# A two-layer decoder trunk on one core: its setup written in another order

## The chip, the core and the metric

The kernel runs on one core of a Trainium2 chip, as one program without collectives. Its time is device microseconds (us) of one execution. TensorE multiplies matrices; VectorE (DVE in the profile), ScalarE (ACT) and GpSimd (POOL) do the elementwise work; SyncE (SP) and ScalarE issue the DMAs. Every engine works off its own instructions in the order in which they stand, and waits at an instruction until what it depends on is done. PEld are TensorE's weight loads, which run beside its matmuls.

## What is computed

The input is 512 tokens of width 1024, in float32. The reference normalises them and runs two layers on them:

```python
h = layer_norm(x, ln_in_g, ln_in_b)
for l in range(DEPTH):                       # 2
    mix = token_mix(h, positions, ...)       # pooling, convolution and sparse attention, gated and merged
    h = layer_norm(DEEPNORM_ALPHA * h + mix, ln1_g[l], ln1_b[l])
    ffn = conv_ffn(h, ...)
    h = layer_norm(DEEPNORM_ALPHA * h + ffn, ln2_g[l], ln2_b[l])
```

`token_mix` begins with one projection of h, whose columns are the inputs of all three branches. Among them are the key of a sparse-attention indexer and its eight query heads. Keys and queries are rotated by angles that come from `positions` (`rope`); the indexer scores every visible key for every query, and the 128 best are kept.

## The kernel before

A float32 product is done in three passes over a high and a low part: a value is copied to a rounded `hi` (ScalarE), the rest `lo = value - hi` is a subtraction, and hi·hi, lo·hi and hi·lo are added in PSUM (`proj`, lines L289, L290, L291). Weights come in 246 chunks of 128x1024 through `Weights`: a DMA into one of two `w_raw` buffers (L70), the copy `w_hi` on ACT (L74), the subtraction `w_lo` (L78) on DVE, or as two halves on POOL for chunks named in `W.side`. There are four hi/lo pairs. So chunk i+2 can be loaded once chunk i is split, and chunk i+4 can be split once TensorE is done with chunk i.

Tokens are four blocks of 128. `setup` does, block by block: statistics of x (`stats`), mean and variance, the power -0.5 on POOL (L177), the normalisation in two halves of 512 (L197), four transposes per half (L200), scale and shift into a tile `gbt` of the four-buffer pool `gb` (three of four on ACT, L208, the last on DVE, L205), then `hT_hi` on ACT (L212) and `hT_lo` on DVE (L112). After block 1 and after block 3 `mix_head.block` multiplies the last two blocks by the first three weight chunks: chunk 0 (indexer key, bank v), chunk 1 (attention key) and chunk 2 (pooling), banks s. 24 products of 256 columns per chunk and pair of blocks make 144. Last stand the rotation angles: positions, a chain of eleven small DVE operations, a sine on ACT, eight products that spread it over partitions, and the tables `sinT` (ACT) and `cosT` (DVE).

Layer 0 starts with `rotate` of the indexer key (`ki`), the attention key (`k`) and the four query tiles (`qi0` to `qi3`, chunks 3 to 6): ACT reads the product into `t` (L424, L425, L440, L455), issues four DMAs that swap halves (L405), POOL multiplies by `sinT` (L409), DVE by `cosT` (L408), and DVE adds (L410). Indexer scores follow (`mask`, L475, L477), then the top-128 search on DVE. Later each gate chunk frees its PSUM bank through DVE (L728).

The order on each engine is set by a list scheduler of the tile framework, which also adds the waits. `add_manual_dep(..., ISSUE_ORDER)` fixes the order of two instructions without a wait of its own. The scheduler reuses eight DMA completion counters (lanes, `DMAHW0` to `DMAHW7`): a DMA that takes a lane waits until the DMA that had it last has landed.

Of the kernel before, what the change touches and what calls it, by code (L numbers as in the profile page):

```python
# [15 lines left out]
P = 128  # L16
D = 1024
L = 512
NB = 4
# [35 lines left out]
class Weights:  # L55
    def __init__(self, tc, w, raw_pool, split_pool, look, nchunk):
        self.tc, self.nc, self.w = tc, tc.nc, w
        self.raw_pool, self.split_pool = raw_pool, split_pool
        self.look = look
        self.n = nchunk  # L60
        self.emitted = 0
        self.used = 0
        self.ready = []
        self.side = set()

    def emit(self, upto):
        nc = self.nc
        while self.emitted < min(upto, self.n):
# [21 lines left out]
def trunk_kernel(ctx, tc, x, positions, w, poolw, params, lnv, cons, out):  # L90
# [20 lines left out]
    def split_lo(lo, src, hi, eng=None):  # L111
        (eng or V).tensor_tensor(out=lo, in0=src, in1=hi.bitcast(F32), op=ALU.subtract)  # L112

# [1 line left out]
    h = const.tile([P, NB, D], F32, name="h")  # L115
    xv = x[0].rearrange("(b p) d -> p b d", p=P)
    par = const.tile([P, DEPTH, NPAR], F32, name="par")
    nc.scalar.dma_start(out=par[:, 0, PO_LN:NPAR], in_=params[:, 0, PO_LN:NPAR])
# [7 lines left out]
    cst = const.tile([P, 37], F32, name="cst")  # L126
    nc.scalar.dma_start(out=cst, in_=cons)
# [31 lines left out]
    class Norm:  # L159
        def __init__(self, i, last=False):  # L160
# [3 lines left out]
            self.tr = [None] * NB  # L164

# [5 lines left out]
        def apply(self, b):  # L171
# [5 lines left out]
            G.tensor_tensor(out=rs, in0=ve, in1=mhalf, op=ALU.pow)  # L177
# [17 lines left out]
            for half in range(2):  # L195
# [3 lines left out]
                for k in range(4):  # L199
                    self.tr[b] = T.transpose(pt[:, k * P:(k + 1) * P], hb[:, k * P:(k + 1) * P], ident)  # L200
                y = g_slot().rearrange("p (k t) -> p k t", k=4)
# [11 lines left out]
                split_lo(lo, y, hi, G if half in LN_POOL else V)  # L213
# [9 lines left out]
    class Head:  # L223
# [3 lines left out]

        def block(self, b):
            if self.wts is None:
                n = len(self.c0s)  # L230
                self.wts = [W.take(look=n - 1 - i) for i in range(n)]
                self.os = [bank(t) for t, _ in zip(("v", "s", "s"), self.c0s)]
            if b % 2 == 1:
                for o, wt, c0 in zip(self.os, self.wts, self.c0s):
                    in_part(o, wt, c0, max(c0, (b - 1) * P), (b + 1) * P)

    def setup():
        norm = Norm(0)
        for b in range(NB):
            for c in range(2):  # L240
                norm.stats(b, c)
            norm.apply(b)
            mix_head.block(b)
        V.tensor_scalar(half_par[:, :, 0:41], par[:, :, PO_B:PO_B + 41], 0.5, None, op0=ALU.mult)
        V.tensor_scalar(half_par[:, :, 41:45], par[:, :, PO_CG:PO_CG + 4], 0.5, None, op0=ALU.mult)
        with tc.tile_pool(name="rt", bufs=1) as rt:
            sel = rt.tile([P, NB, NB, 32], F32R, name="sel")
            G.tensor_copy(sel, ident.rearrange("p (b f) -> p b f", b=NB).unsqueeze(2).to_broadcast([P, NB, NB, 32]))
            pi = rt.tile([P, P], I32, name="pi")
            for b in range(NB):  # L250
                nc.sync.dma_start(out=pi[32 * b:32 * b + 32, :],
                                    in_=positions[:, b * P:(b + 1) * P].to_broadcast([32, P]))
            both = rt.tile([P, 2, P], F32, name="both")
            ang, cang = both[:, 0, :], both[:, 1, :]
            V.tensor_scalar(ang, pi, cst[:, 0:1], None, op0=ALU.mult)
            n = rt.tile([P, P], F32, name="n")
            magic = 12582912.0
            V.tensor_scalar(n, ang, 1.0 / (2 * PI), magic, op0=ALU.mult, op1=ALU.add)
            V.tensor_scalar(n, n, magic, None, op0=ALU.subtract)
            for c in (6.28125, 0.00193023681640625, 5.066394805908203e-06,  # L260
                      2 * PI - 6.28125 - 0.00193023681640625 - 5.066394805908203e-06):
                V.scalar_tensor_tensor(out=ang, in0=n, scalar=-c, in1=ang, op0=ALU.mult, op1=ALU.add)
            V.tensor_scalar(ang, ang, 3.1415925, -3.1415925, op0=ALU.min, op1=ALU.max)
            V.scalar_tensor_tensor(out=cang, in0=ang, scalar=-1.0, in1=ang, op0=ALU.mult, op1=ALU.min)
            V.tensor_scalar(cang, cang, PI / 2, None, op0=ALU.add)
            A.activation(both, both, AF.Sin)
            b_hi = rt.tile([P, 2, P], F32R, name="b_hi")
            b_lo = rt.tile([P, 2, P], F32R, name="b_lo")
            A.activation(b_hi, both, AF.Copy)
            split_lo(b_lo, both, b_hi)  # L270
            for half in range(2):
                o = bank("p").rearrange("p (b v t) -> p b v t", b=2, v=2)
                for b in range(2):
                    w = sel[:, 2 * half + b].rearrange("p r f -> p (r f)")
                    T.matmul(o[:, b], w, b_hi, start=True, stop=False)
                    T.matmul(o[:, b], w, b_lo, start=False, stop=True)
# [3 lines left out]
        return norm  # L280

    def proj(o, wt, col, xs, kts):
# [3 lines left out]
        for i, (wc, xc) in enumerate(kts):  # L286
# [4 lines left out]
            T.matmul(o, wl, xh(xc), start=False, stop=(i == n - 1))  # L291

    def in_part(o, wt, c0, a, b):
        proj(o[:, a - c0:b - c0], wt, 0,
             (lambda k: hT_hi[:, k, a:b], lambda k: hT_lo[:, k, a:b]),
# [620 lines left out]
```

## Time and profile before

| | us |
|---|---|
| median of 3 runs (1559.52 to 1560.57) | 1559.91 |
| profiled execution, first to last instruction | 1558.4 |
| TensorE busy | 1498.9 |
| DVE busy | 999.1 |
| ACT busy | 682.4 |
| POOL busy | 534.9 |

The profiled execution's own time is its span; what the runs add around a span is taken as the difference to the median, 1.5 us. TensorE is busy for 96% of the span. A share like this is a mean over stages: in the first 20 us TensorE is busy for 4.04 us only, and between 120 and 200 us DVE is the engine without idle time. The stage that is touched is the first 45 us, and what hangs on it up to about 240 us.

### The profile page before, as it was taken

The numbers are of one execution on the slowest core, as the hardware profiler recorded it, in microseconds if no ns is written. First come the engines' busy times: TensorE is split into PE (matmuls) and PEld (weight loads), VectorE is DVE, ScalarE is ACT, GpSimd is POOL, SyncE is SP. The second block draws the span as 40 slices with busy tenths as digits, with TensorE's granted clock in tenths as the row PEclk, the third lists the DMA queues.
The fourth block names the chain that finished last, engine by engine and source line by source line (L and its number), as shares of the span: only waits on it lengthen the run. The fifth ranks groups of instructions, "written<-read, shape, count | busy, mean of one in ns | idle before, by whom it ended". The sixth has DMA issues, their size and how long they took to land.

```text
span 1558.4 us, 18612 instructions
## 1 busy us (share of the span) xinstructions
PE 1498.9 (96%) x6850; PEld 1215.8 (78%) x6850; DVE 999.1 (64%) x1596; ACT 682.4 (44%) x1064; POOL 534.9 (34%) x395
## 2 busy tenths in 40 slices
PE   5998999999999999999999988999999999999997
PEld 5876677777888888888898756777878788888885
DVE  6799997655666555533268999966557655555234
ACT  5665635452444444421255664455325444443110
POOL 2356932208471110100134677231374611010004
PEclk9999999999999999999999999999999999999998
DMA  4432221223233333333234222312323433332331
GB/s 146 142 92 75 68 89 61 68 68 109 81 116 111 99 95 95 95 95 103 86 103 120 72 67 82 95 57 66 108 81 99 132 101 101 96 95 83 107 98 65
DMA packets 45018, 145.02 MB, mean 93 GB/s; under 512 B 6144, under 2 KB 7808, under 8 KB 44928
## 3 DMA queue, kind: packets, MB, share of 16 engines
q1 hardware_dynamic: 37632, 133.55, 27.8%
q10 hardware_dynamic: 7296, 10.29, 2.3%
q8 instruction: 54, 0.88, 0.2%
q14 instruction: 36, 0.29, 0.1%
HBM read 137.00 MB, written 2.10 MB: 89 GB/s over the span
## 4 chain that ended last, share of the span: by engine, by line
PE 71%; DVE 12%; POOL 7%; issue 4%; ACT 2%; DMA 2%; ACTq 0%; POOLq 0%; DVEq 0%
PE pb_a L289 15%; PE pb_a L290 15%; PE pb_a L291 15%; POOL h L221 3%; POOL h L220 2%; PE pb_a L318 2%; PE pb_a L317 2%; PE pb_a L316 2%; DVE mask L477 2%; DVE w_lo L78 2%; DVE mask L485 2%; PE pb_p L318 2%; PE pb_p L317 2%; PE pb_p L316 1%; PE pb_s L318 1%
## 5 line engine op out<-in xcount | busy, mean ns | idle before, releaser
L289 PE MATMUL pb_a<-hT_hi,w_hi 128*128 128x512 f32 (+1 forms) x1264 | 497.8, 394 | 26.0 <-DVE part L728 15.9
L78 DVE TENSOR_TENSOR w_lo<-w_raw,w_hi 128x1024 fp32r<-128x1024 f32 x210 | 287.0, 1367 | 342.7 <-ACT w_hi L74 341.9
L291 PE MATMUL pb_a<-hT_hi,w_lo 128*128 128x512 f32 (+1 forms) x1264 | 496.2, 393 | 0.0
L290 PE MATMUL pb_a<-hT_lo,w_hi 128*128 128x512 f32 (+1 forms) x1264 | 496.0, 392 | 0.0
L74 ACT ACTIVATE w_hi<-w_raw 128x1024 fp32r<-128x1024 f32 x246 | 260.4, 1058 | 434.9 <-PE pb_a L290 190.2
L289 PEld LDWEIGHTS pb_a<-hT_hi,w_hi 128*128 128x128 f32 x1264 | 239.5, 190 | 80.0 <-DVE part L728 19.6
L291 PEld LDWEIGHTS pb_a<-hT_hi,w_lo 128*128 128x128 f32 x1264 | 239.5, 189 | 49.1 <-issue 2.0
L290 PEld LDWEIGHTS pb_a<-hT_lo,w_hi 128*128 128x128 f32 x1264 | 239.5, 189 | 48.4 <-issue 1.3
L78 POOL TENSOR_TENSOR w_lo<-w_raw,w_hi 128x512 fp32r<-128x512 f32 x72 | 101.6, 1433 | 290.1 <-ACT w_hi L74 290.1
L799 POOL TENSOR_TENSOR fu<-fu 128x512 f32<-128x512 f32 x44 | 61.2, 1391 | 356.6 <-DVE fu L793 356.6
L589 POOL TENSOR_TENSOR cv<-cv,cvt 128x512 f32<-128x512 f32 x92 | 143.4, 1559 | 47.1 <-ACT cvt L588 42.4
L588 ACT ACTIVATE cvt<-cv,par 128x512 f32<-128x512 f32 x92 | 65.1, 720 | 35.7 <-POOL cv L589 35.5
L798 ACT ACTIVATE fu<-fu 128x512 f32<-128x512 f32 x44 | 27.8, 631 | 81.7 <-DVE fu L793 81.7
L793 DVE SCALAR_TENSOR_TENSOR fu<-pb_a,par,fu 128x510 f32<-128x510 f32 x82 | 61.4, 749 | 2.7
L790 ACT ACTIVATE fu<-pb_a,par 128x512 f32<-128x512 f32 x82 | 62.3, 760 | 0.0
L791 DVE SCALAR_TENSOR_TENSOR fu<-pb_a,par,fu 128x511 f32<-128x511 f32 x82 | 60.9, 743 | 0.0
L220 POOL TENSOR_TENSOR h<-h,gbt 128x512 f32<-128x512 f32 x32 | 51.9, 1652 | 18.5 <-DMA gbt<-in_lnv_dram 18.5
L484 DVE MAX8 m<-mask 128x8 f32<-128x256 f32 (+2 forms) x96 | 52.8, 553 | 1.1
L748 POOL TENSOR_TENSOR part<-part,t 128x512 f32<-128x512 f32 x16 | 23.5, 1470 | 87.4 <-DVE t L747 68.4
L208 ACT ACTIVATE gbt<-pb_a,par 128x128 f32<-128x128 f32 x96 | 35.6, 466 | 39.6 <-PE pb_a L200 39.6
L682 ACT ACTIVATE qa<-qa,mx 128x128 f32<-128x128 f32 (+3 forms) x64 | 35.6, 556 | 38.4 <-DVE mx L679 37.5
L485 DVE MATCH_REPLACE8 mask<-m,mask 128x256 f32<-128x256 f32 (+2 forms) x96 | 51.9, 541 | 0.0
(290 smaller groups left out, 2570.5 us busy)
## 6 DMA issues: line engine op xcount, KB each, us to landing
w_raw<-in_w_dram SPq DMA_DIRECT2D x246, 512.0 KB, 3.6
gbt<-in_lnv_dram ACTq DMA_DIRECT2D x20, 256.0 KB, 3.6
h<-in_x_dram SPq DMA_DIRECT2D x4, 512.0 KB, 5.4
t<-t ACTq DMA_DIRECT2D x32, 64.0 KB, 2.0
out_dram<-h SPq DMA_DIRECT2D x8, 256.0 KB, 2.0
part<-t ACTq DMA_DIRECT2D x32, 48.0 KB, 3.2
part<-t ACTq DMA_DIRECT2D x16, 64.0 KB, 4.2
par<-in_params_dram SPq DMA_DIRECT2D x2, 143.5 KB, 6.4
```

The source lines that it names most:

```text
L74: nc.scalar.activation(hi, raw, AF.Copy)
L78: eng.tensor_tensor(out=lo[:, cs], in0=raw[:, cs], in1=hi[:, cs].bitcast(F32), op=ALU.subtract)
L220: G.tensor_tensor(out=hb, in0=hb, in1=gb[0][c], op=ALU.mult)
L289: T.matmul(o, wh, xh(xc), start=(i == 0), stop=False)
L290: T.matmul(o, wh, xl(xc), start=False, stop=False)
L291: T.matmul(o, wl, xh(xc), start=False, stop=(i == n - 1))
L317: T.matmul(po[b], lh(k, b), wl, start=False, stop=False)
L318: T.matmul(po[b], ll(k, b), wh, start=False, stop=(k == nk - 1))
L485: V.match_replace(out=sc, in_to_replace=m8, in_values=sc, imm_value=FILL)
L588: A.activation(tm, hp[c][:, i:i + L], AF.Copy, scale=tap(i))
L589: G.tensor_tensor(out=pacc, in0=pacc, in1=tm, op=ALU.add)
L790: A.activation(t, o, AF.Identity, bias=par[:, l, PO_FB + ct:PO_FB + ct + 1], scale=tapw(2))
```

## The change

All four blocks' statistics and powers come first. POOL's weight splits are held behind the last power (`W.after`), and chunk 2's split goes to POOL too (`range(3)`). Then blocks 0 and 1 are normalised and transposed, the three products on them start, and block 2's and 3's transposes are placed behind the first and the second chunk's product. The angles follow the last `hT_lo`. The positions move from SP's queue to ACT's, ahead of the norm's parameters, into a buffer of pool `gb`; the fourth position load takes the lane of x's first block, the parameters the lane of the first position load.

```diff
-                    eng.tensor_tensor(out=lo[:, cs], in0=raw[:, cs], in1=hi[:, cs].bitcast(F32),
-                                      op=ALU.subtract)
+                    sub = eng.tensor_tensor(out=lo[:, cs], in0=raw[:, cs], in1=hi[:, cs].bitcast(F32),
+                                            op=ALU.subtract)
+                    if self.after is not None and self.emitted in self.side:
+                        self.tc.add_manual_dep(sub.ins, self.after.ins.name, ISSUE_ORDER)
...
+    nc.scalar.dma_start(out=cst, in_=cons)
+    pi = g_slot(I32)[:, 0:P]
+    for b in range(NB):
+        nc.scalar.dma_start(out=pi[32 * b:32 * b + 32, :], in_=positions[:, b * P:(b + 1) * P].to_broadcast([32, P]))
     nc.scalar.dma_start(out=par[:, 0, PO_LN:NPAR], in_=params[:, 0, PO_LN:NPAR])
...
     def setup():
         norm = Norm(0)
-        for b in range(NB):
-            for c in range(2):
-                norm.stats(b, c)
-            norm.apply(b)
-            mix_head.block(b)
...
+            for b in range(NB):
+                for c in range(2):
+                    norm.stats(b, c)
+                pw = norm.scale(b)
+            W.after = pw
+            for b in range(2):
+                norm.apply(b)
+            mix_head.begin()
+            W.after = None
+            for i in range(3):
+                end = mix_head.part(i, 0)
+                if i + 2 < NB:
+                    norm.apply(i + 2)
+                    tc.add_manual_dep(norm.t0[i + 2].ins, end.ins.name, ISSUE_ORDER)
+            for i in range(3):
+                mix_head.part(i, 2)
+            ang_hi, ang_lo, sel = angles(rt, norm.lo)
...
+        first = V.tensor_scalar(ang, pi, cst[:, 0:1], None, op0=ALU.mult)
+        tc.add_manual_dep(first.ins, after.ins.name, ISSUE_ORDER)
...
-    W.side.update(range(2))
+    W.side.update(range(3))
```

POOL at the start, from the last of its constants (`sel`) on; `ln_rs` is the power, `w_lo` a half of a weight split. Before:

```order
L137 AFFINE_SELECT ctri<-ctri 128x128
L248 CAST sel<-ident 128x512
L177 TENSOR_TENSOR ln_rs<-ln_ve,mhalf 128x1 x2
L78 TENSOR_TENSOR w_lo<-w_raw,w_hi 128x512 x2
L177 TENSOR_TENSOR ln_rs<-ln_ve,mhalf 128x1 x2
L78 TENSOR_TENSOR w_lo<-w_raw,w_hi 128x512 x2
```

After:

```order
L143 AFFINE_SELECT ctri<-ctri 128x128
L298 CAST sel<-ident 128x512
L185 TENSOR_TENSOR ln_rs<-ln_ve,mhalf 128x1 x4
L79 TENSOR_TENSOR w_lo<-w_raw,w_hi 128x512 x6
L604 MEMSET cv 128x30 x2
```

The last two powers no longer stand behind chunk 0's split, and six halves follow without anything between them.

DVE, from the third and fourth blocks' variances on. Before:

```order
L197 TENSOR_SCALAR h<-h,ln_mv,ln_rs 128x512 x2
L173 BN_AGGR ln_mv<-ln_st 128x2
L175 TENSOR_SCALAR ln_ve<-ln_mv 128x1
L205 TENSOR_SCALAR gbt<-pb_a,par 128x128
L175 TENSOR_SCALAR ln_ve<-ln_mv 128x1
L112 TENSOR_TENSOR hT_lo<-gbt,hT_hi 128x4x128
L255 TENSOR_SCALAR both<-pi,cst 128x128
```

After:

```order
L212 TENSOR_SCALAR h<-h,ln_mv,ln_rs 128x512 x2
L181 BN_AGGR ln_mv<-ln_st 128x2
L183 TENSOR_SCALAR ln_ve<-ln_mv 128x1
L222 TENSOR_SCALAR gbt<-pb_a,par 128x128
L183 TENSOR_SCALAR ln_ve<-ln_mv 128x1
L222 TENSOR_SCALAR gbt<-pb_a,par 128x128
L212 TENSOR_SCALAR h<-h,ln_mv,ln_rs 128x512 x4
L115 TENSOR_TENSOR hT_lo<-gbt,hT_hi 128x4x128
L222 TENSOR_SCALAR gbt<-pb_a,par 128x128
L115 TENSOR_TENSOR hT_lo<-gbt,hT_hi 128x4x128
```

The four normalisations of blocks 2 and 3 now stand ahead of every `hT_lo`, also those of blocks 0 and 1, and the angles' operations have left this place.

ACT, from the end of the norm to the first read of a product (`t<-pb_v`), with the waits of each; `w_hi` are chunks 4, 5 (before) and 4, 5, 6 (after). Before:

```order
L212 ACTIVATE hT_hi<-gbt 128x4x128 [waits DVE_49]
L278 ACTIVATE sinT<-pb_p,cst 128x256 [waits DMAHW3_49,PE_49]
L278 ACTIVATE sinT<-pb_p,cst 128x256 [waits PE_49]
L74 ACTIVATE w_hi<-w_raw 128x1024 [waits DMAHW0_49,PE_49,Pool_49]
L424 ACTIVATE t<-pb_v,par 64x512 [waits DMAHW4_49,DMAHW3_49,DMAHW5_49,DMAHW2_49,PE_49]
L425 ACTIVATE t<-pb_v,par 64x512
L427 ACTIVATE t<-pb_v,par 8x512
L74 ACTIVATE w_hi<-w_raw 128x1024 [waits DMAHW1_49,PE_49,Pool_49]
```

After:

```order
L229 ACTIVATE hT_hi<-gbt 128x4x128 [waits DVE_49]
L313 ACT_TABLE_LOAD
L313 ACTIVATE both<-both 128x256 [waits DVE_49]
L75 ACTIVATE w_hi<-w_raw 128x1024 [waits DMAHW0_49,PE_49,Pool_49]
L316 ACTIVATE b_hi<-both 128x256 [waits Activation_49]
L75 ACTIVATE w_hi<-w_raw 128x1024 [waits DMAHW1_49,PE_49,Pool_49]
L75 ACTIVATE w_hi<-w_raw 128x1024 [waits DMAHW2_49,PE_49,Pool_49]
L291 ACTIVATE sinT<-pb_p,cst 128x256 [waits PE_49] x2
L463 ACTIVATE t<-pb_v,par 64x512 [waits DVE_49]
```

Sine tables and the first read of a product have moved behind the copies of chunks 4, 5 and 6.

## Rows read from the trace of the kernel before

**Rows 1.** The page: span.

```profile
span 1558.4 us, 18612 instructions
```

**Rows 2.** TensorE's waits, whole trace: releaser, us in total, times, longest.

```profile
PE pb_a L289 <- DVE part L728: 15.9, 10, 2.9
```

**Rows 3.** Busy time by engine in stretches of 20 us.

```profile
180.00:200.00 20.00, 17.31 (x71) 13.51 (x71) 19.72 (x34) 11.73 (x18) 19.17 (x14) 0.96 0.24 78
...
240.00:260.00 20.00, 20.00 (x90) 14.99 (x88) 13.39 (x41) 10.43 (x24) 5.11 (x4) 1.00 0.26 79
```

**Rows 4.** TensorE's instructions in order of time: start, us, what, [idle before].

```profile
19.90 1.94 PE L200 MATMUL pb_a<-ident,h 128*128 128x128 f32 x8 [5.67 <-issue]
...
22.86 0.58 PE L290 MATMUL pb_v<-hT_lo,w_hi 128*128 128x256 f32 x1
...
23.89 0.42 PE L291 MATMUL pb_v<-hT_hi,w_lo 128*128 128x256 f32 x1
24.10 0.41 PE L289 MATMUL pb_v<-hT_hi,w_hi 128*128 128x256 f32 x1
...
42.16 0.28 PE L290 MATMUL pb_s<-hT_lo,w_hi 128*128 128x256 f32 x1
42.28 0.28 PE L291 MATMUL pb_s<-hT_hi,w_lo 128*128 128x256 f32 x1
```

**Rows 5.** POOL in order of time.

```profile
12.65 2.95 POOL L78 TENSOR_TENSOR w_lo<-w_raw,w_hi 128x512 fp32r<-128x512 f32 x2 [2.03 <-ACT w_hi L74]
...
16.59 2.60 POOL L78 TENSOR_TENSOR w_lo<-w_raw,w_hi 128x512 fp32r<-128x512 f32 x2
```

**Rows 6.** ACT in order of time; ACTq are DMA issues.

```profile
5.11 1.28 ACT L208 ACT_TABLE_LOAD   x1 [5.11 <-DMA par<-in_params_dram]
9.42 2.20 ACT L208 ACTIVATE gbt<-pb_a,par 128x128 f32<-128x128 f32 x6 [3.03 <-PE pb_a L200]
...
37.47 0.47 ACT L278 ACTIVATE sinT<-pb_p,cst 128x256 f32<-128x256 f32 x1 [2.53 <-PE pb_p L276]
...
39.89 1.06 ACT L74 ACTIVATE w_hi<-w_raw 128x1024 fp32r<-128x1024 f32 x1 [1.10 <-PE pb_v L290]
40.86 0.67 ACT L424 ACTIVATE t<-pb_v,par 64x512 f32<-64x512 f32 x1
...
46.64 1.06 ACT L74 ACTIVATE w_hi<-w_raw 128x1024 fp32r<-128x1024 f32 x1 [1.91 <-DMA w_raw<-in_w_dram]
...
62.27 2.44 ACTq L405 DMA_DIRECT2D part<-t  x4
```

**Rows 7.** DVE in order of time.

```profile
4.85 1.29 DVE L169 BATCH_NORM_STATS2 ln_st<-h 128x6 f32<-128x512 f32 x2 [3.99 <-DMA h<-in_x_dram]
...
13.12 1.35 DVE L112 TENSOR_TENSOR hT_lo<-gbt,hT_hi 128x512 fp32r<-128x512 f32 x1
...
22.13 0.68 DVE L112 TENSOR_TENSOR hT_lo<-gbt,hT_hi 128x512 fp32r<-128x512 f32 x1
...
40.98 1.23 DVE L78 TENSOR_TENSOR w_lo<-w_raw,w_hi 128x1024 fp32r<-128x1024 f32 x1 [1.74 <-ACT w_hi L74]
...
72.13 1.11 DVE L475 TENSOR_SCALAR mask<-u,wq 128x256 f32<-128x256 f32 x1
```

**Rows 8.** DMA issues up to 60 us: times, KB each, us to landing.

```profile
part<-t ACTq DMA_DIRECT2D x8, 64.0 KB, 4.1
...
par<-in_params_dram ACTq DMA_DIRECT2D x1, 40.0 KB, 4.3
```

**Rows 9.** The normalisation, all 32 of it: ns min/median/max.

```profile
L197 DVE TENSOR_SCALAR h<-h,ln_mv,ln_rs x32: 531/542/550, 7.7 to 1189.9; 128x512 f32<-128x512 f32 x32
```

**Rows 10.** DVE and POOL at 785 us, in order of time.

```profile
785.04 0.54 DVE L197 TENSOR_SCALAR h<-h,ln_mv,ln_rs 128x512 f32<-128x512 f32 x1
785.24 1.50 POOL L78 TENSOR_TENSOR w_lo<-w_raw,w_hi 128x512 fp32r<-128x512 f32 x1 [0.69 <-ACT w_hi L74]
```

**Rows 11.** SP's DMA issues in order of time.

```profile
42.24 0.33 SPq L70 DMA_DIRECT2D w_raw<-in_w_dram  x1
```

More of the change, by code (lines that the diff above doesn't have):

```diff
@@ L64, in __init__ @@
         self.side = set()
+        self.after = None
     def emit(self, upto):
@@ L226, in __init__, with begin, part @@
             self.wts = None
+        def begin(self):
+            n = len(self.c0s)
+            self.wts = [W.take(look=n - 1 - i) for i in range(n)]
+            self.os = [bank(t) for t, _ in zip(("v", "s", "s"), self.c0s)]
+        def part(self, i, b):
+            c0 = self.c0s[i]
+            return in_part(self.os[i], self.wts[i], c0, max(c0, b * P), (b + 2) * P)
         def block(self, b):
             if self.wts is None:
-                n = len(self.c0s)
-                self.wts = [W.take(look=n - 1 - i) for i in range(n)]
@@ L232, in block @@
-                self.os = [bank(t) for t, _ in zip(("v", "s", "s"), self.c0s)]
+                self.begin()
             if b % 2 == 1:
-                for o, wt, c0 in zip(self.os, self.wts, self.c0s):
-                    in_part(o, wt, c0, max(c0, (b - 1) * P), (b + 1) * P)
+                for i in range(len(self.c0s)):
+                    self.part(i, b - 1)
     def setup():
         norm = Norm(0)
-        for b in range(NB):
-            for c in range(2):
-                norm.stats(b, c)
-            norm.apply(b)
-            mix_head.block(b)
@@ L250, in setup @@
             for b in range(NB):
[L251 to L264, printed above, removed]
@@ L280, in setup, with angles @@
         return norm
+    def angles(rt, after):
+        sel = rt.tile([P, NB, NB, 32], F32R, name="sel")
+        G.tensor_copy(sel, ident.rearrange("p (b f) -> p b f", b=NB).unsqueeze(2).to_broadcast([P, NB, NB, 32]))
+        both = rt.tile([P, 2, P], F32, name="both")
+        ang, cang = both[:, 0, :], both[:, 1, :]
+        first = V.tensor_scalar(ang, pi, cst[:, 0:1], None, op0=ALU.mult)
+        tc.add_manual_dep(first.ins, after.ins.name, ISSUE_ORDER)
+        n = rt.tile([P, P], F32, name="n")
+        magic = 12582912.0
+        V.tensor_scalar(n, ang, 1.0 / (2 * PI), magic, op0=ALU.mult, op1=ALU.add)
+        V.tensor_scalar(n, n, magic, None, op0=ALU.subtract)
+        for c in (6.28125, 0.00193023681640625, 5.066394805908203e-06,
+                  2 * PI - 6.28125 - 0.00193023681640625 - 5.066394805908203e-06):
+            V.scalar_tensor_tensor(out=ang, in0=n, scalar=-c, in1=ang, op0=ALU.mult, op1=ALU.add)
+        V.tensor_scalar(ang, ang, 3.1415925, -3.1415925, op0=ALU.min, op1=ALU.max)
+        V.scalar_tensor_tensor(out=cang, in0=ang, scalar=-1.0, in1=ang, op0=ALU.mult, op1=ALU.min)
+        V.tensor_scalar(cang, cang, PI / 2, None, op0=ALU.add)
+        A.activation(both, both, AF.Sin)
+        b_hi = rt.tile([P, 2, P], F32R, name="b_hi")
+        b_lo = rt.tile([P, 2, P], F32R, name="b_lo")
+        A.activation(b_hi, both, AF.Copy)
+        split_lo(b_lo, both, b_hi)
+        return b_hi, b_lo, sel
     def proj(o, wt, col, xs, kts):
@@ L290, in proj @@
             T.matmul(o, wh, xl(xc), start=False, stop=False)
-            T.matmul(o, wl, xh(xc), start=False, stop=(i == n - 1))
+            end = T.matmul(o, wl, xh(xc), start=False, stop=(i == n - 1))
+        return end
     def in_part(o, wt, c0, a, b):
-        proj(o[:, a - c0:b - c0], wt, 0,
-             (lambda k: hT_hi[:, k, a:b], lambda k: hT_lo[:, k, a:b]),
-             [(k * P, k) for k in range(KT)])
+        return proj(o[:, a - c0:b - c0], wt, 0,
+                    (lambda k: hT_hi[:, k, a:b], lambda k: hT_lo[:, k, a:b]),
+                    [(k * P, k) for k in range(KT)])
     def in_tile(c0=0, tag="a"):
```

39 lines of the change are left out of this document (20 added, 19 removed).

## Prediction

> **What bounds the kernel now.** I read the page first: the span is 1558.4 us [rows 1]. Then the waits of TensorE: its largest is for VectorE, 15.9 us at the gate stage L728 [rows 2]. Then the busy times by stretch: at 180 to 200 us VectorE works 19.72 of 20 us and TensorE 17.31; from 240 us on TensorE works without a break and VectorE has room (13.39 of 20) [rows 3]. So layer 0 has three parts: a start in which TensorE stands still, a stretch up to about 240 us that VectorE's work bounds, and a rest that TensorE bounds. What is won or lost at the start reaches the end only as far as it moves the beginning of VectorE's dense stretch, and TensorE with it.
>
> Last I read the first 72 us engine by engine. TensorE stands still 5.67 us before block 2's transposes at 19.90; the first product with a low part of tokens starts at 22.86, and the last of the 144 head products at 42.28 [rows 4]. POOL's row shows why block 2 was late: chunk 0's split holds POOL from 12.65 for 2.95 us, and the powers of blocks 2 and 3 stand behind it [rows 5]. That is the wait which the change takes away. What comes late next is the question.
>
> **The change, part by part.**
>
> *Parameters behind positions.* Before, ACT waits for the norm's parameters until 5.11, loads its table (1.28) and starts scaling block 0 at 9.42 [rows 6]. In the new order four position loads stand ahead of the parameters on ACT's queue. The last of them takes the lane of x's first block, which lands at 4.85 [rows 7]; with two issues of about 0.45 us (an estimate: ACT's issues in rows 6 take 0.61) the parameters go out at 5.7 at the earliest, land 4.3 us later [rows 8], and after the table load ACT starts at 11.3, 1.9 us later. Bounds: 0 (if the load lands before the first transposes all the same) and 3.9 (landing 2 us slower beside x).
>
> *Statistics first, six splits in one piece.* ACT then needs 2.20 us for block 0's scaling and about 1 us for chunk 0's copy [rows 6], so POOL's first split starts at about 15, not at 12.65. From there six halves follow, and VectorE has blocks 2 and 3's normalisations (four of 0.54, [rows 9]) and block 0's two `hT_lo` in front of block 1's. How the two engines share is in the rows: `hT_lo` takes 0.68 undisturbed and 1.35 beside a split [rows 7]; two halves take 2.60, and 2.95 with one whole `hT_lo` between them [rows 5]. One half and one such VectorE operation thus need 1.30 + 0.35 = 1.65 us together. Whether the normalisation is held as well, no row of before shows: none of its 32 is longer than 0.55 [rows 9]. But the one half that began beside one took 1.50, 0.2 more than its usual 1.30 [rows 10], so they do exclude each other, and I take it as held. Two of the four pass before POOL starts; the other two and block 0's two `hT_lo` make four rounds of 1.65, from 15.4 to 22.0. Block 1's scaling has waited for a `gbt` buffer meanwhile (the positions occupy one of the four), so its first `hT_lo` ends at about 23.2, where before it ended at 22.8. If the normalisation is not held, two rounds of 1.30 go, and it is 20.6.
> The Trainium skill speaks to the same point: "Advanced Engine Details and Errata", section "VectorE Performance Modes", says that VectorE's second port to SBUF is shared with GpSimd and that two-port instructions and GpSimd's block each other, and gives source and destination in SBUF as a condition of such a mode. By that page the four normalisations are held and the sum is the one below; by the 32 undisturbed durations alone TensorE's term would be about 2.6 us smaller.
>
> *TensorE.* From its first low product at 23.2 it has 143 products of 256 columns at 0.12 us, as from 42.16 to 42.28 [rows 4], = 17.2, and 16 transposes at 0.12 = 1.9 (before, 12 of these lay in the idle time ahead of 22.86). It starts after a pause of some 8 us: the row spacing at 23.89 to 24.10 is 0.21 us, the lower of the clock's two levels, and became 0.12 about 4.5 us after 19.90. In the new order some 3.4 us of products run at that spacing, which costs 1.5. With 0.4 for block 3's last tiles the head ends at 23.2 + 17.2 + 1.9 + 1.5 + 0.4 = 44.2. Eight products of the angles (1.0) and one of chunk 3 (0.2), done before 42.40 until now, follow. TensorE is then at 45.4 where it was at 42.4: **+3.0**. Bounds: +0.4 (normalisations not held) and +4.7 (parameters 2 us later).
>
> *Angles last.* ACT's new order puts the copies of chunks 4, 5 and 6 ahead of `sinT`, and `sinT` ahead of the first read of a product. Chunk 4's copy waits for TensorE's last use of chunk 0, as it does now at 39.89 [rows 6]: 44.2 less the 23 products behind it (2.8) = 41.4. Then copy 1.06, split 1.23 on VectorE [rows 7], and only now may chunk 6 be loaded; that takes 4.4 us today (issue 42.24, copy at 46.64) [rows 6, 11]; copy 1.06, `sinT` twice 0.47. The first `t` is read at 41.4 + 1.1 + 1.2 + 4.4 + 1.1 + 0.9 = 50.1 instead of 40.86, 9.2 us later.
> Most of it comes back, since what follows today is itself full of waits for chunks (1.91 at 46.64). ACT issues 24 swapping DMAs up to the last rotation, at 0.61 (four take 2.44, [rows 6]), 14.6 us in all. Between them it stands still for chunk 8 (1.1) and for the sums of `ki`, `k`, `qi0` and `qi1` (2.1, 1.2, 1.9, 2.8; each is landing 4.1 [rows 8], product on POOL 1.3 and sum 0.7, less the issues beside it), and 1.0 us is left to the score. So the first `mask` is at 50.1 + 14.6 + 9.1 + 1.0 = 74.8 instead of 72.13 [rows 7]: +2.7. If POOL and VectorE hold each other at four of these sums as in the row of 1.35, it is 2.0 us more: +4.7. Both durations occur in rows 7, so I take the middle, **+3.6**. From that row on both builds leave VectorE the same work: five sums and the splits up to chunk 11 stand ahead of it in either order.
>
> *What costs and gives nothing.* Chunk 2's split on POOL takes 1.23 us off VectorE, but VectorE waits for chunk 6 right after it; that cover gone, it would be a gain of 1.2. The angles' eleven operations lie in VectorE's wait for TensorE's head.
>
> *Sum.* TensorE's 3.0 and VectorE's 3.6 are not added; VectorE's is the later one, and TensorE waits for it at L728. Span 1558.4 + 3.6 = 1562.0. The runs' median is 1.5 us above the profiled span, so the time is **1563.5**, 0.23% more. Less than 0.2% (3.1 us) can hardly be told from no change here.
>
> **Rivals.**
> 1. *The rotations don't catch up.* If the six sums come late by the full 9.2 us and VectorE waits through it, the dense stretch begins 6 to 9 us late: 1566 to 1569. For it: ACT works off its issues in order, and every standstill above is a minimum. Against: chunks 7 to 10 are ready earlier than today.
> 2. *It hides.* The normalisations are not held, or the parameters land early: TensorE +0.4, and the rotations regain as above: -1 to +2 us, 1559 to 1562. For it: none of 32 normalisations was stretched. Against: the stretched half at 785.24.
> 3. *Faster: the dense stretch is sorted anew.* The list scheduler places VectorE's instructions differently up to about 340 us. If fewer search steps stand ahead of the gate sums L728, part of TensorE's 15.9 us of waits for them [rows 2] goes. I count half of these for layer 0, 8 us, since both layers run the same program; 6 to 8 of them gone outweigh the 3.6 and leave -2 to -5: 1555 to 1558. It decides once more than 3.6 us of waits vanish. For it: in the new order the second branch's gates have fewer VectorE instructions ahead of them. Against: ahead of the sums L728 themselves stand nearly the same ones.
>
> **How the numbers follow.** The forecast (with +1 to +6 as its own range, 1561 to 1566) gets 0.46; rival 1 0.20, rival 2 0.19, rival 3 0.15. Of the forecast's share 0.27 lies above +3.1 us and 0.19 below; rival 1 is slower, rival 2 the same, rival 3 faster but for 0.01. Slower 0.47, same 0.39, faster 0.14. The range leaves out the outer half of rivals 1 and 3: 1556 to 1569.
>
> **What would show it.** Right: ACT's first scaling at about 11, six POOL halves from 15 on with stretched VectorE rows between them, the first low product at 23, `t` at 50 behind chunk 6's copy with a wait on its DMA, the first `mask` at 75. Wrong: a first low product before 21, `sinT` ahead of chunk 6's copy, or `mask` before 73; and, for rival 3, less than 4 us of L728 waits in layer 0 together.

## The result and the profile after

The changed kernel takes 1569.87 us (median of 5, 1568.17 to 1571.23), the kernel before 1559.91 on the same chip: ratio 1.0058 [1.0046, 1.007], slower by 10.0 us between the medians. The ratio is not the quotient of these two medians (1.0064); by it the difference is 9.0 us. The forecast was 1563.5 us, in a range of 1556 to 1569. The profiled execution is the median one. Its span, which answers to [rows 1], has grown by 9.7:

```profile
span 1568.1 us, 18596 instructions
```

Most of what the prediction says of the setup can be seen. ACT's row of the changed kernel (start, us, what) answers to [rows 6]: the parameters go out at 5.96 behind four position loads and the first scaling starts at 11.27. Chunk 6's copy waits 3.63 us for its load, and `sinT` and the first `t` stand behind it, at 48.16 instead of 40.86.

```profile
1.18 3.89 ACTq L125 DMA_DIRECT2D gbt<-in_positions_dram  x4
5.96 0.35 ACTq L126 DMA_DIRECT2D par<-in_params_dram  x1
9.98 1.28 ACT L225 ACT_TABLE_LOAD   x1 [9.98 <-DMA par<-in_params_dram]
11.27 2.20 ACT L225 ACTIVATE gbt<-pb_a,par 128x128 f32<-128x128 f32 x6
...
46.48 1.06 ACT L75 ACTIVATE w_hi<-w_raw 128x1024 fp32r<-128x1024 f32 x1 [3.63 <-DMA w_raw<-in_w_dram]
47.45 0.82 ACT L291 ACTIVATE sinT<-pb_p,cst 128x256 f32<-128x256 f32 x2
48.16 0.67 ACT L463 ACTIVATE t<-pb_v,par 64x512 f32<-64x512 f32 x1
```

POOL's row answers to [rows 5], and DVE's row below it to [rows 7, 9]. POOL splits from 14.49 on, and the four normalisations beside it take 3.81 us, where four alone took 2.2 (4 x 0.542). The third of the three splits stands apart, at 23.01: POOL waits 2.56 us for its copy on ACT. The first `mask` is at 75.56, 3.4 us later than before.

```profile
14.49 2.86 POOL L79 TENSOR_TENSOR w_lo<-w_raw,w_hi 128x512 fp32r<-128x512 f32 x2 [0.75 <-ACT w_hi L75]
17.52 2.93 POOL L79 TENSOR_TENSOR w_lo<-w_raw,w_hi 128x512 fp32r<-128x512 f32 x2 [0.16 <-ACT w_hi L75]
```

```profile
13.83 3.81 DVE L212 TENSOR_SCALAR h<-h,ln_mv,ln_rs 128x512 f32<-128x512 f32 x4
...
75.56 1.15 DVE L514 TENSOR_SCALAR mask<-u,wq 128x256 f32<-128x256 f32 x1
```

TensorE's row from 12 to 43 us answers to [rows 4]: no stall of 5.67 us ahead of block 2's transposes any more, but one of 7.07 ahead of the first head product. The first product with a low part comes at 21.97, the last of the head's at 42.98 instead of 42.28.

```profile
21.15 0.58 PE L327 MATMUL pb_v<-hT_hi,w_hi 128*128 128x256 f32 x1 [7.07 <-ACT hT_hi L229]
...
21.97 0.58 PE L328 MATMUL pb_v<-hT_lo,w_hi 128*128 128x256 f32 x1
...
42.98 0.28 PE L329 MATMUL pb_s<-hT_hi,w_lo 128*128 128x256 f32 x1
```

That makes 3.4 us at the first `mask`. Where the rest comes from can be seen first in the list of TensorE's waits, which answers to [rows 2] (L728 is L767 now). The sums of the gates cost somewhat more, and a wait has come that before did not have at all: for `qa_hi`, the copy of an attention output.

```profile
PE pb_a L327 <- DVE part L767: 17.6, 8, 4.6
...
PE pb_a L327 <- ACT qa_hi L742: 2.6, 1, 2.6
```

Here is its place, first on TensorE after, then on TensorE before. `pb_v<-qb,vst` are the last products of layer 0's attention; `pb_a<-qa_hi` needs their result through ACT and DVE.

```profile
351.52 0.39 PE L736 MATMUL pb_v<-qb,vst 128*128 128x512 f32 x1
354.55 1.65 PE L327 MATMUL pb_a<-qa_hi,w_hi 128*128 128x512 f32 x3 [2.63 <-ACT qa_hi L742]
355.99 0.63 PE L328 MATMUL pb_a<-qa_lo,w_hi 128*128 128x512 f32 x1
...
357.27 0.45 PE L328 MATMUL pb_a<-qa_lo,w_hi 128*128 128x512 f32 x1
357.56 0.40 PE L329 MATMUL pb_a<-qa_hi,w_lo 128*128 128x512 f32 x1
```

```profile
344.92 0.40 PE L697 MATMUL pb_v<-qb,vst 128*128 128x512 f32 x1
345.16 0.39 PE L289 MATMUL pb_a<-hT_hi,w_hi 128*128 128x512 f32 x1
...
347.68 0.39 PE L291 MATMUL pb_a<-hT_hi,w_lo 128*128 128x512 f32 x1
347.90 0.63 PE L289 MATMUL pb_a<-qa_hi,w_hi 128*128 128x512 f32 x2
```

Before, twelve products of a gate (345.16 to 347.90, 2.74 us) stand behind the last one with `vst` and cover that chain. After, they have been done earlier and nothing is left to cover it. ACT's row shows what TensorE waits for (DVE's addition, 0.69 from 353.14, lies between the two):

```profile
352.45 0.59 ACT L738 ACTIVATE o<-pb_v 64x512 f32<-64x512 f32 x1
353.86 0.63 ACT L742 ACTIVATE qa_hi<-o 128x512 fp32r<-128x512 f32 x1 [0.83 <-DVE o L739]
```

In this execution the stall costs more than its length. The seven products from 354.55 to 357.56 take 3.01 us, at 0.23 each they would take 1.6, so 1.4 more are lost. The windows of the changed kernel (columns as in [rows 3]; the granted clock is the third number from the end) show the clock of this stretch at 0.91, where before has 1.00 there and no idle time; of the two levels, 1.2 and 2.4 GHz, those products ran near the lower. The same stall in p3 below is not followed by such products.

```profile
340.00:360.00 20.00, 17.37 (x74) 13.83 (x74) 7.28 (x10) 6.29 (x10) 0.00 (x0) 0.91 0.21 74
```

So the account along the program, in the two profiled executions, reads: +3.4 us at the first `mask`. At the last product with `vst`, 351.52 against 344.92 is +6.6, but before has 2.74 us of products still to do there; at equal work it is +3.9. The wait makes it +6.6 at the first product with `qa_hi` (354.55 against 347.90), the slow products +8.0 (the first product of the down projection behind it, L355, stands at 378.42, its counterpart before at 370.39). From there to 900 us it stays at 8.0 to 8.6, with the instructions in the same order; the last 1.2 come up in layer 1's VectorE-bound stretch, where the granted clock is 0.95 (900 to 1000 us) against 0.97.

### The profile page after: what moved, and what is told of

Same layout as the page of the kernel before. It is cut to its first block, busy times and chain, and to the rows that moved or that the text cites. A ratio compares the mean times of both kernels' runs of the same rounds, so it can differ in the third digit from the quotient of the medians.

```text
span 1568.1 us, 18596 instructions
## 1 busy us (share of the span) xinstructions
PE 1504.5 (96%) x6850; PEld 1218.2 (78%) x6850; DVE 1001.4 (64%) x1595; ACT 681.8 (43%) x1064; POOL 538.0 (34%) x397
## 4 chain that ended last, share of the span: by engine, by line
PE 78%; DVE 8%; POOL 7%; issue 3%; ACT 2%; DMA 1%; ACTq 0%; POOLq 0%; DVEq 0%
PE pb_a L327 17%; PE pb_a L328 17%; PE pb_a L329 17%; POOL h L238 3%; POOL h L237 2%; PE pb_a L357 2%; PE pb_a L356 2%; PE pb_a L355 2%; PE pb_p L357 2%; PE pb_p L356 1%; PE pb_p L355 1%; PE pb_s L357 1%; PE pb_s L356 1%; PE pb_s L355 1%; PE pb_s L715 1%
## 5 line engine op out<-in xcount | busy, mean ns | idle before, releaser
L79 POOL TENSOR_TENSOR w_lo<-w_raw,w_hi 128x512 fp32r<-128x512 f32 x74 | 106.9, 1466 | 277.3 <-ACT w_hi L75 277.3
L628 POOL TENSOR_TENSOR cv<-cv,cvt 128x512 f32<-128x512 f32 x92 | 143.2, 1556 | 55.5 <-ACT cvt L627 49.4
```

Source lines behind the costliest of these rows:

```text
L79: sub = eng.tensor_tensor(out=lo[:, cs], in0=raw[:, cs], in1=hi[:, cs].bitcast(F32), op=ALU.subtract)
L628: G.tensor_tensor(out=pacc, in0=pacc, in1=tm, op=ALU.add)
```

## The experiments

In most of them the order behind the setup is held. The setup is left to the scheduler; behind it every engine's instructions are chained with order-only edges, up to the down projection at about 400 us, in an order that was read from a built kernel. `ORDER` has one row of instruction numbers for each engine, counted from the first `t` on; instructions have the same numbers in both kernels there.

```diff
     norm = setup()
+    mark = len(nc.cur_bb.bb.instructions)
...
+    for row in ORDER:
+        for a, b in zip(row, row[1:]):
+            tc.add_manual_dep(seq[f"I-{base + b}"], f"I-{base + a}", ISSUE_ORDER)
```

All times are medians, beside runs of the kernel before on the same chip. First `t`, first `mask` and the last column (the first product of layer 0's down projection, against 370.39 in the kernel before) are from the profiled run.

| run | setup | order behind it | first t | first mask | us against before | ratio | down projection |
|---|---|---|---|---|---|---|---|
| before | before | before | 40.86 | 72.13 | 0 | 1 | 0 |
| changed | changed | changed | 48.16 | 75.56 | +10.0 | 1.0058 [1.0046, 1.007] | +8.0 |
| p1 | changed | before | 47.26 | 77.78 | +8.0 | 1.0048 [1.0035, 1.006] | +5.9 |
| p2 | changed | changed to the mask, then before | 48.35 | 75.69 | +4.3 | 1.0026 [1.0017, 1.0036] | +2.7 |
| p3 | before | before to the mask, then changed | 41.35 | 72.73 | +4.1 | 1.0025 [1.0016, 1.0035] | +3.4 |
| p4 | changed, angle products first on TensorE | before | 43.95 | 75.04 | +5.0 | 1.0036 [1.0022, 1.005] | +2.7 |
| s1 | parameters first, angles free | before | 42.92 | 73.66 | +0.8 | 1.0004 [0.9995, 1.0013] | +1.3 |
| s2 | angles free | before | 43.02 | 74.32 | +3.0 | 1.0017 [1.0008, 1.0025] | +2.2 |
| s3 | parameters first | changed to the mask, then before | 45.90 | 72.13 | +2.1 | 1.0011 [1.0002, 1.002] | -0.4 |
| s4 | before, statistics lead | before | 38.39 | 72.24 | -0.6 | 0.9997 [0.9989, 1.0006] | -0.3 |
| q1 | changed | changed to the attention's end, then before | 48.28 | 75.76 | +4.6 | 1.0035 [1.0022, 1.0049] | +4.4 |
| q2 | changed | changed; before from mask to attention's end | 48.61 | 76.19 | +9.2 | 1.0059 [1.0046, 1.0071] | +7.9 |
| n1 | parameters first | scheduler's own | 45.68 | 72.89 | +6.6 | 1.0041 [1.0028, 1.0053] | +5.1 |
| n2 | as s4 | scheduler's own | 37.98 | 71.07 | -1.3 | 0.9988 [0.9979, 0.9997] | -1.5 |

Behind that product VectorE, ScalarE and GpSimd have the same order in all of these kernels, and still the profiled executions fall back by another 0.1 to 4.8 us against before from there to their ends. So one or two us of the whole time say little on the order; that column says more.

**Start or sorting: p2 and p3.** The edit is the one above, with these rows in `ORDER`:

```diff
+ORDER  # p2: the changed kernel's order up to its first mask, then the order of before
+ORDER  # p3: the order of before up to its first mask, then the changed kernel's
```

> The changed kernel; up to its first mask every engine keeps the changed kernel's order, behind it the rest is held in the order of the kernel before. So the late start stays whole (first t at 48.2, first mask at 75.6) and only the sorting behind it is undone. Theory A: +3.4 us against before, 1563 to 1564 us, no wait for qa_hi at 352 us. Theory B: 1568 to 1571 us, as the changed kernel.

> The mirror image: the kernel before with its own setup and its own order up to its first mask (at 72.1 us), behind it the order of the changed kernel. The start is not late at all; only the sorting is the changed kernel's. Theory A: +6 us, 1565 to 1567 us, with the wait for qa_hi near 350 us. Theory B: 1560 us, no change.

p2 gives +4.3, p3 +4.1, together 8.4 of the 10.0. Theory A holds in its kind: there are two losses, and each is there without the other. Its split was off (3.4 and 6 expected), and p2 lies above its 1563 to 1564. Theory B falls: p3 starts as before and still loses. Its trace has the wait, with a start that is not late. But here the products behind the wait come at 0.27 and soon at 0.23 us, and the granted clock of the stretch stays at 1.00:

```profile
PE pb_a L289 <- ACT qa_hi L703: 2.6, 1, 2.6
```

```profile
351.16 0.97 PE L289 MATMUL pb_a<-qa_hi,w_hi 128*128 128x512 f32 x3 [2.63 <-ACT qa_hi L703]
351.96 0.42 PE L290 MATMUL pb_a<-qa_lo,w_hi 128*128 128x512 f32 x1
352.23 0.40 PE L291 MATMUL pb_a<-qa_hi,w_lo 128*128 128x512 f32 x1
```

```profile
340.00:360.00 20.00, 17.37 (x80) 13.74 (x79) 8.53 (x13) 7.16 (x10) 2.22 (x2) 1.00 0.23 68
```

So the wait comes with the order; the slow products behind it come in some executions (the changed kernel's, q2's and n1's profiled ones) and not in others. At the down projection the changed kernel is 5.3 us behind p2, with the same start: 1.1 of it come up between `mask` and the end of the attention, 2.8 with the wait and 1.4 with the slow products.

**Where the sorting costs: q1 and q2.** The same edit, with these rows:

```diff
+ORDER  # q1: the changed order up to the first transpose of the attention's last part, then before
+ORDER  # q2: changed to the first mask, before from there to that transpose, then changed
```

> The changed kernel with its own order up to the first transpose of the attention's last part (at 243.8 us), behind it the order of before. The stretch that VectorE bounds (75 to 240 us) is thus sorted as changed; only the end of the attention is not: twelve of the products that need no attention stand behind the last product with vst again. Theory C (the sorting costs by the end of the attention: TensorE waits 2.6 us for qa_hi and then does its next products at twice the spacing, 1.6 us): 1565 to 1567.5 us, about 4 below the changed kernel. Theory D (the sorting costs in the dense stretch, 120 to 220 us): the wait is gone but the time stays at 1568 to 1571 us.

> The mirror image of the run before it: changed order up to the first mask, the order of before from there to the first transpose of the attention's last part, behind that the changed order, with no product left behind the last product with vst. Theory C: the wait of 2.6 us for qa_hi is there and the time is 1567 to 1570 us, about 3 to 4 above p2. Theory D: 1564.5 to 1566.5 us, as p2.

q2 decides for theory C: it has the order of before in the whole stretch that VectorE bounds, and loses 9.2 us where p2 lost 4.3; the two intervals are apart (its 1570.25 us lie just above theory C's range). q1 points the same way, less firmly. It keeps the changed order in that stretch, and its median loses 4.6 us instead of 10.0, but its five runs form two groups, 1564.9 to 1565.6 (three) and 1569.4 and 1569.8, and the second is what theory D expects. The profiled run is of the second group. Its trace is clearer: the wait is gone and the down projection starts at +4.4 instead of +8.0. The rest is lost later, 2.6 us of it at 1234 us, in layer 1, where a wait for VectorE is followed by slow products; p2 has that wait without them. q1's two rows, then p2's:

```profile
1234.55 0.61 PE L327 MATMUL pb_a<-hT_hi,w_hi 128*128 128x512 f32 x1 [2.01 <-DVE fu L832]
1234.96 0.63 PE L328 MATMUL pb_a<-hT_lo,w_hi 128*128 128x512 f32 x1
```

```profile
1231.98 0.47 PE L327 MATMUL pb_a<-hT_hi,w_hi 128*128 128x512 f32 x1 [2.00 <-DVE fu L832]
1232.29 0.39 PE L328 MATMUL pb_a<-hT_lo,w_hi 128*128 128x512 f32 x1
```

So at the down projection the end of the attention is worth 3.6 us (changed kernel against q1) to 5.2 us (q2 against p2). In q1 TensorE (row of 352 us) goes from a gate's product to `qa_hi` without a break:

```profile
352.06 0.39 PE L329 MATMUL pb_a<-hT_hi,w_lo 128*128 128x512 f32 x1
352.29 0.63 PE L327 MATMUL pb_a<-qa_hi,w_hi 128*128 128x512 f32 x2
```

and q2 has the stall, at 354.16:

```profile
354.16 0.97 PE L327 MATMUL pb_a<-qa_hi,w_hi 128*128 128x512 f32 x3 [2.63 <-ACT qa_hi L742]
```

**What makes the start late: p1 and p4.** p1 holds the whole order behind the setup to that of before, so that `t` is read ahead of chunk 6's copy.

```diff
+ORDER  # p1: the order of before, from the first t on
```

> The changed kernel, with every instruction behind the setup (from the first read of a head product on) held in the order that it has in the kernel before, on every engine. ACT then reads the first t ahead of chunk 6's copy again; statistics, splits on POOL, positions ahead of the parameters and angles last stay as changed. Theory A (a late start of 3 to 4 us at the first mask, and about 6 us more from the way in which the rest of layer 0 is sorted): first t at about 45 instead of 48.2, first mask at +1 to +2 us against before, TensorE's wait of 2.6 us for qa_hi at 352 us gone, 1561 to 1563 us. Theory B (all 10 us follow from the late start, whatever the sorting): half the lateness of t gives half the loss, about 1565 us.

Missed by far: `t` comes only 0.9 us earlier, `mask` at 77.78, and the time is +8.0, though the wait for `qa_hi` is gone. Why `mask` comes 2.1 us later than in p2, with a `t` that is 1.1 earlier, no run separates. ACT's row says why `t` is so late: chunk 6's copy is gone from ahead of `sinT`, but `sinT` waits for TensorE.

```profile
46.53 0.84 ACT L291 ACTIVATE sinT<-pb_p,cst 128x256 f32<-128x256 f32 x2 [5.53 <-PE pb_p L289]
```

The products of the angles stand among and behind 20 products of chunk 3 on TensorE, in p1 as in the changed kernel (the expectations of p4 say 23). So `sinT` had two bounds there that ended within 0.2 us of each other: these products (the last one starts at 47.40) and the copy (46.48 + 1.06 = 47.54). Taking one away shows nothing. p4 takes both away:

```diff
+    for e in turned:                       # the second products of the angles, L289
+        tc.add_manual_dep(seq[f"I-{base + ORDER[0][0]}"], e.ins.name, ISSUE_ORDER)
```

> As p1 (changed setup, behind it the order of before), with one thing more: TensorE does the eight products of the angles ahead of chunk 3's products, not behind 23 of them. In p1 the sine tables waited 5.53 us for these products, so that t came at 47.3 although chunk 6's copy was no longer ahead of it. Theory A1 (the start is late by sinT, which had two bounds that ended together: chunk 6's copy on ACT at 47.5 and the angle products on TensorE at 47.4): with both gone sinT comes at 43 to 44, t at 44 to 45, the first mask at 73 to 75, the time is 1561 to 1564 us. Rival (t is not what the rest waits for): mask stays at 77 to 78 and the time at 1567 to 1570 us.

```profile
43.21 0.84 ACT L291 ACTIVATE sinT<-pb_p,cst 128x256 f32<-128x256 f32 x2 [2.07 <-PE pb_p L289]
43.95 0.67 ACT L463 ACTIVATE t<-pb_v,par 64x512 f32<-64x512 f32 x1
```

`t` is at 43.95, as theory A1 expects but for 0.05. `mask` comes 2.7 us earlier than in p1, for a `t` that is 3.3 earlier, but at 75.04 it just misses the 73 to 75 expected, and the time of +5.0 lies above theory A1's and below its rival's. `t` matters, and it is not all.

**The two parts of the setup: s1, s2, s3.** s2 takes away the edge that holds the angles back, s3 puts the parameters in front, s1 does both and moves the positions back to SP's queue.

```diff
-        tc.add_manual_dep(first.ins, after.ins.name, ISSUE_ORDER)       # s2, s1
...
+    nc.scalar.dma_start(out=par[:, 0, PO_LN:NPAR], in_=params[:, 0, PO_LN:NPAR])   # s3, s1
     nc.scalar.dma_start(out=cst, in_=cons)
```

> The changed kernel's statistics first, its six splits in one piece on POOL and its products ahead of the transposes of blocks 2 and 3, but parameters first on ACT's queue, positions on SP's, and the angles free to come early, as before; the order behind the setup is that of the kernel before. If late parameters and late angles are what makes the start late (theory A's start), ACT starts scaling at 9.4, sinT stands well ahead of the first t, the first mask is within 1 us of before and the time is 1559 to 1561 us. If the splits in one piece and the order of the products are what costs (a rival for the start), TensorE's head ends 1.5 us or more later than before and the time is 1562 us or more.

> The changed kernel without the edge that holds the first angle operation behind the last hT_lo, so the angles come early; parameters stay behind the positions, and the order behind the setup is that of before. If angles last is the whole of the start's loss: sinT before 40, t at 42 to 43.5, first mask at 73 to 74, 1560 to 1563 us. If the parameters behind the positions cost their 1.9 us on top: mask at 75, 1563 to 1565 us.

> As p2 (the changed kernel's order up to its first mask, behind it that of before), with the norm's parameters first on ACT's queue, ahead of the constants and positions. ACT starts scaling at about 9.4 instead of 11.2. If the late parameters cost what the prediction took (1.9 us of the start): first mask at 73.5 to 74.5, 1562 to 1564 us. If POOL's six halves and block 1's wait set TensorE's head, or the late angles do (theory A1): mask within 1 us of 75.7, 1564 to 1566 us.

s1 lies between its two answers, nearer the second. ACT starts scaling at 9.49 and `sinT` stands at 35.86, far ahead of `t`, but TensorE's last head product starts at 44.83, 2.5 us later than before, `mask` is 1.5 late, and 1561.92 us is just below the second answer's 1562. In time that is +0.8, hardly told from none. Splits in one piece and the order of the products are not what makes the head late by themselves, since s3 has both and its head is early.

s3 is the surprise. With the angles as late as in the changed kernel and `t` at 45.90, 5 us later than before, the first `mask` is at 72.13, as early as before. ACT's row of s3 at the start, then DVE's at the `mask`:

```profile
7.04 1.28 ACT L225 ACT_TABLE_LOAD   x1 [7.04 <-DMA cst<-in_cons_dram]
9.67 2.20 ACT L225 ACTIVATE gbt<-pb_a,par 128x128 f32<-128x128 f32 x6 [1.35 <-PE pb_a L215]
```

```profile
72.13 1.10 DVE L514 TENSOR_SCALAR mask<-u,wq 128x256 f32<-128x256 f32 x1
```

One DMA of 40 KB at the head of its queue gives back the whole lateness at `mask` (75.69 in p2): ACT starts 1.5 us earlier than in p2, TensorE's last head product starts at 40.78 instead of 43.12, and the rotations catch up 5 us of `t`. So `mask` is earlier than either side of the expectation has it, while the 1562.91 us lie in the range of the first. But it is not the DMA alone. The setup is left to the scheduler, and it sorts s3's setup anew: block 0's first `hT_lo` stands ahead of all four normalisations of blocks 2 and 3 and its second ahead of two of them, and block 0's first `hT_hi` stands ahead of chunk 0's copy. What the earlier load gives and what this order gives is not separated. In time it is 2.2 us between s3 and p2, whose intervals overlap a little. The +2.1 us that are left in s3 do not come from the start: its trace is 0.4 us ahead of before at layer 0's down projection and level (+0.1) at layer 1's, at 1133.70; behind it, it falls back to +1.6. s2's `mask` lies between its two expectations and its time of +3.0 in the second: the angles free bring `sinT` to 35.96, but TensorE's head then ends at 44.92, with the angle operations among those of blocks 2 and 3 on DVE. So the parts are not a sum: with the parameters first, freeing the angles makes `mask` later (s1 73.66, s3 72.13), with the parameters late it makes it earlier (s2 74.32, p2 75.69). The difference in order (s1 and s2 have the order of before behind the setup) is part of that, and is not separated. Two pairs have the same order behind the setup: p1 and s2 differ in the edge of the angles (`mask` 77.78 and 74.32, +8.0 and +3.0 us), s2 and s1 in the place of the parameters and in the queue and buffer of the positions (74.32 and 73.66, +3.0 and +0.8).

**The wait that the change is about: s4 and n2.** s4 is the kernel before with statistics leading and POOL's splits behind the last power, and with the angles' code placed between the blocks so that they stay early.

```diff
         for b in range(NB):
             for c in range(2):
                 norm.stats(b, c)
-            norm.apply(b)
-            mix_head.block(b)
+            W.after = norm.scale(b)
+        norm.apply(0)
...
```

> The kernel before with only the wait taken away that the change is about: statistics of all blocks lead, POOL's splits stand behind the last power (four halves, as before), angles early, positions and parameters as before, transposes as before, the order behind the setup that of before. TensorE's 5.67 us ahead of block 2's transposes must go. If that wait set the end of TensorE's head: head end at 40 to 41 instead of 42.3, first mask 1 to 2 us earlier, 1558.5 to 1560 us. If the head is set by block 1's hT_lo and the splits on POOL all the same: mask within 1 us of 72.1, 1560 to 1562 us.

The same time as before (0.9997). The 5.67 us of [rows 4] did not go, contrary to what both sides of the expectation took for sure. TensorE's row at block 2's transposes, then DVE's:

```profile
20.87 1.97 PE L211 MATMUL pb_a<-ident,h 128*128 128x128 f32 x8 [5.20 <-DVE gbt L216]
```

```profile
13.94 4.75 DVE L208 TENSOR_SCALAR h<-h,ln_mv,ln_rs 128x512 f32<-128x512 f32 x4
```

Blocks 2 and 3 have their powers early now, so their normalisations come ahead of block 1's last scalings on DVE, and beside POOL's four halves (5.60 us from 14.21) they take 4.75 us. Block 2's transposes then wait for a PSUM tile that those scalings have to free. The wait has another releaser now and nearly the same length. The `mask` is within 0.1 us of before, as the second side of the expectation says.

The kernel before shows that there, too, the powers were only a part of it. POOL's row and then DVE's:

```profile
15.56 1.07 POOL L177 TENSOR_TENSOR ln_rs<-ln_ve,mhalf 128x1 f32<-128x1 f32 x2
```

```profile
16.73 2.61 DVE L262 SCALAR_TENSOR_TENSOR both<-n,both 128x128 f32<-128x128 f32 x2
19.26 0.53 DVE L197 TENSOR_SCALAR h<-h,ln_mv,ln_rs 128x512 f32<-128x512 f32 x1
```

The powers end at 16.63, and block 2's first normalisation starts at 19.26, behind two operations of the angles that take 2.61 us beside POOL's second split (two of them take 0.60 in s4, without a split beside them).

**Own order: n1 and n2.** The kernels of s3 and s4 with no `ORDER` at all.

```diff
-    for row in ORDER:
-        for a, b in zip(row, row[1:]):
-            tc.add_manual_dep(seq[f"I-{base + b}"], f"I-{base + a}", ISSUE_ORDER)
```

> The changed kernel with nothing but the norm's parameters first on ACT's queue, and its order left to the scheduler, which makes it the changed kernel's (apart from some products behind 380 us). If start and sorting add up (s3: mask as early as before, +2 us; sorting +4): 1565 to 1567 us, with the wait for qa_hi. If the sorting costs only behind a late start: 1561 to 1563 us.

> s4 (the kernel before with statistics leading, splits on POOL behind the last power, angles early) with its order left to the scheduler instead of held to that of before. It is sorted a third way; ten products stand behind the last product with vst, so theory C expects no wait for qa_hi and 1559 to 1562 us. Theory D gives no number; a time over 1563 us without that wait would say that the dense stretch's own sorting costs.

n1 is sorted as the changed kernel behind the setup, has the wait for `qa_hi` (2.6 us), and loses 6.6: its start costs little (`mask` +0.8) and the sorting 4.5, against s3. Its 1567.61 us lie 0.6 above the sum's range, so start and sorting add up, and the rival of its expectation falls. n2 is sorted a third way, keeps products for the end of the attention, has no such wait, and lies as expected: at 0.9988 [0.9979, 0.9997] it is 1.3 us faster than the kernel before, just clear of no change; its `mask` is at 71.07.

## Why the prediction was right, and where it was short

The direction, slower, was right, and for a reason that it names, but that reason is less than half of the loss; the size was short by 6.4 us, and the time lies 0.9 above the range.

- *The wait at the outset.* POOL's row was taken as the reason for TensorE's 5.67 us. It is about half of it: 2.6 us lie behind the powers, where VectorE does the angles beside POOL, and with the powers early the wait stayed (s4, 5.20).
- *Parameters behind positions.* Forecast 11.3 for ACT's start, measured 11.27. What it weighs was underrated: it entered only as the beginning of POOL's splits. With the parameters first, most of the late start is gone (3.4 us between the changed kernel and n1 in time, 3.5 at `mask` between p2 and s3), though both kernels' setups are also sorted anew by it.
- *Statistics first, six splits.* POOL's first split forecast at 15, measured 14.49; the normalisations were taken as held by POOL, and were (3.81 us for four). Six halves in one piece were four, and two from 23.01 on. The Trainium skill's "Advanced Engine Details and Errata", section "VectorE Performance Modes", says that GpSimd's instructions and two-port ones of VectorE block each other; the traces here agree, with 3.81 and 4.75 us for four that take 2.2 alone.
- *TensorE.* First low product forecast 23.2, measured 21.97, since block 0's second `hT_lo`, forecast to end at 22.0, ended at 21.0, and block 1's first follows it. Head end forecast 44.2, measured 43.1, so +0.7 against before and not +1.8. The upper bound of this term, +4.7, is not what its own steps give (3.0 and 2.0 are 5.0). The low spacing lasted from 21.15 to 26.36: 20 products at 0.21 from 21.97 on cost 1.8, forecast 1.5. That this is the lower clock level is read from the spacing alone: the granted clock of 20 to 25 us reads 1.00 in both kernels.
- *Angles last.* `t` forecast at 50.1, measured 48.16; `mask` forecast at 75.7 (+3.6), measured 75.56 (+3.4). That the sum came out is luck: `t` was taken 1.9 us too late, and from `t` to `mask` it takes 27.4 us where the middle of the forecast had 25.6. And only half of the mechanism is in it: the prediction names chunk 6's copy as what holds `sinT`, and p1 shows TensorE's own products of the angles as a second bound of the same length. And s3 shows that a `t` 5 us late can be made good before `mask`.
- *Sum: the failing term.* The prediction carried `mask`'s 3.6 us to the end, on "From that row on both builds leave VectorE the same work". VectorE's work is the same; TensorE's cover at the end of the attention is not. Sorting anew stood only in rival 3, as a gain from L728 waits. Those waits grew in layer 0, from 6.9 to 9.6 us between 75 and 400 us, and what decided was a place outside of them: the end of the attention, with 2.63 us of wait and, in some executions, 1.4 of slow products. So the term that failed is the sorting behind the setup, which the sum puts at nothing and rival 3 at a gain. p3 against before, q2 against p2 and n1 against s3 each show it by itself, as a loss of 4 to 5 us.
- *Rival 1* (1566 to 1569) has nearly the time, but not the cause: the rotations did catch up.
- *What stays open:* the last 1.2 us in layer 1, whose order is the same (the changed kernel's own runs differ by 3.1 us), and what s3 loses behind layer 1's down projection; when a stall is followed by slow products; and how the late start is shared between the parameters, the angles and the setup's own order.

## What to carry to other kernels

Where a list scheduler sets the order, an edit at the start can also re-sort stretches far behind it, and that can cost as much as the edit itself. Hold the order behind the edit to that of before, and the two losses can be measured apart. Where the edit's own stretch is left to the scheduler (s3 here), its effect and that of the new order there stay mixed. In a stretch that TensorE bounds, look at the end of each dependent phase for independent products that still stand behind it: here a dozen of them covered a chain through two other engines. And a small load that the first instruction of an engine needs belongs ahead of everything that is needed later on the same queue.

## What the runs showed of the hardware

- A normalisation of 128x512 on DVE that takes 0.54 us alone takes 0.95 to 1.19 on average beside POOL's halves (four in 3.81 and in 4.75 us); `hT_lo` took 1.76 and 1.43 there instead of 0.68, and an operation of 128x128 that takes 0.23 otherwise (L305 in the changed kernel's row at 36.71) took 1.28 beside the last half in s4. The 32 in [rows 9] did not show it; the stretched half in [rows 10] did.
- A stall of 2.63 us on TensorE was followed by products at 0.39 to 0.48 instead of 0.23 us for seven products in the changed kernel and for eight in q2, with a granted clock of 0.91 in that stretch of 20 us in both. The same stall in p3 was followed by four at 0.27, with a granted clock of 1.00. A stall of 2.0 us in layer 1 was followed by slow products in q1 (granted clock 0.83 from 1230 to 1240 us) and not in p2 (1.00). What decides between the two no run shows.
- Four position loads of 16 KB hold ACT's queue for 3.89 us, and for 5.29 in s3, where two loads stand ahead of them instead of one. The prediction put the parameters' issue behind them at 5.7; it came at 5.96.
